# A gated-recurrence pass moved by half a slot to a slot, a row sum ahead of a copy from its bank, and one pair's casts on GpSimd

## The chip, the cores and the metric

One core of one Trainium2 chip runs the whole kernel. The metric is device time in microseconds (us) of one execution. A NeuronCore has a matrix engine (TensorE, PE in the profile; its weight loads are PEld), VectorE (DVE), ScalarE (ACT), GpSimd (POOL) and SyncE (SP, which here issues most DMAs). Each engine works through its own queue in order, and semaphores hold an instruction until what it needs is done. TensorE writes into PSUM, which has eight banks of 128 partitions by 512 fp32 numbers; VectorE and ScalarE read it, GpSimd does not.

## The reference, cut to what matters

One encoder layer over 1024 tokens of width 1024:

```
h     = layer_norm(x)
proj  = h @ w_in                     # 1024 -> 5120: q k v z_a u z_b g_a g_b
y_a   = neighbourhood_attention(q, k, v, rpb) * silu(z_a)
u     = centred_depthwise_conv(u)
for d in (forward, reverse):         # RG-LRU, 8 blocks of 64 channels
    r, i  = sigmoid(u @ w_gate + b_gate)
    a     = exp(-8 * softplus(-lam) * r)
    bx    = sqrt(1 - a*a) * i * u    # 1 instead of the root at the first position
    h_d   = scan: h[t] = a[t] * h[t-1] + bx[t]
y_b   = (h_0 + h_1) * silu(z_b)
m     = sigmoid(g_a + b0) * (y_a @ w_ba) + sigmoid(g_b + b1) * (y_b @ w_bb)
out   = layer_norm(2**0.25 * h + m @ w_out)
```

## The kernel before, in words

All matrix products are of fp32 data that is cut into a high and a low part (`hi`, `lo`), so each product is three matmuls (`mm3`, line 136, whose matmul is line 140). Two large stages, the combined input projection and the output projection, use a Strassen-Winograd scheme of seven products in place of eight. The order of all engines' queues is written out by hand.

**The projection stage** (about 81 to 420 us of the span). It handles 17 pairs of column blocks, p0 to p16; each pair has seven products, k0 to k6, in the order `a11 a12 s2 s1 s3 s4 a22`. One product is twelve matmuls and makes one slot: slot 7p+k. The loop over slots is at line 1162. In a slot, in this order: the results of the product before are taken out of PSUM (`evacuate`, line 1086); the high part of a weight for the next pair is cast (`s_hi`, line 474); the steps planned for position 0 of the slot; the squashings (`squash`, line 779); the product; the low parts of weights (`s_lo`, line 479); the stores; a weight sum on VectorE (`s_sum`, line 467); and the steps planned for position 1.

Products share banks: `s2`, `s3` and `a22` are added into the bank of `a11`, and `s4` into that of `s1`. So product k6 of a pair may start only when VectorE has read the state after k4 out of the bank. That read is line 776 (812 for keys, 767 for u), in `evacuate` of slot 7p+5, and appears in the profile as `c<-u,a` (a bank `c` from a copy `u` and the bank `a`; where `u` is taken, `up<-u,a`).

**The gate passes.** The recurrence has eight passes, one for each of four channel tiles and two directions (`gate_stage`, line 874), which begin at slots 21, 31, 42, 52, 63, 73, 84 and 94; they are called pass 0 to pass 7 here. The forward passes are the even ones. A pass consists of steps planned for a slot and a position counted from its beginning: `gates` (TensorE), `sigmoid` (ScalarE, line 892), `gated_input` (GpSimd, line 895), `decay` and `growth` (ScalarE, lines 898 and 902), `square` (ScalarE, line 905), `left` (VectorE, line 908, 1 + a*a times the tanh), `root` (ScalarE, line 911, with a table load), `tables` (ScalarE, line 914, which loads the sigmoid table again), `inputs` (a VectorE memset of one column, line 918, and GpSimd's product, line 919), `scan` (VectorE, line 924). A reverse pass goes on with `fetch`, `total` and two `gated`. The list of times is at lines 941 to 958. A convolution stage (`conv_stage`, line 831; its VectorE taps are line 843) runs beside it.

**Casts of weights.** Per pair, five high parts (`HI_POOL`, line 40) are cast on GpSimd, except for the pairs in `HI_ACT` (line 42), which ScalarE casts. Two low parts per pair are on GpSimd, the others on VectorE (line 134).

**The end.** The output projection ends with the four row blocks p0 to p3 of two halves r. `finished(p, r)` (line 1631) takes the mean and variance of a row block, normalises the two halves of the columns on ScalarE (`normal`, line 1637), scales them on GpSimd (`scaled_on`, line 1642) and stores them. For the block (2, 1) some work is inserted between the small steps of `newton` (line 1589) by `MEANWHILE` (line 1623): there it is a copy by ScalarE of the bank `banksX[3]` (line 1615). VectorE adds the same bank to a row block at line 1700 and takes its statistics at line 1587. Then come two half sums with the last product (`last_piece`, line 1626), the last normalisation (lines 1787 to 1799) and the last stores.

Of the kernel before, what the change touches and what calls it, by code (L numbers as in the profile page):

```python
# [13 lines left out]
ALU = mybir.AluOpType  # L14
# [24 lines left out]
LO_POOL = ("a11", "a22")  # L39
HI_POOL = ("a12", "s2", "s1", "s3", "s4")  # L40
FIRST_POOL = ("a22", "s4")
HI_ACT = (1, 2, 3, 16)
HELD = (18, 32, 37, 39, 60, 81)
U_PAIRS = (1, 6)
BLOCKS = (1, 0, 6, 4, 3, 2, 5, 7)
# [16 lines left out]
def tiled(ap, n):  # L62

    return ap[:, n * HALF:(n + 1) * HALF].rearrange("p (j r c) -> p j r c", r=GR, c=8)


def gridded(ap, n):

    return ap.rearrange("p (r j c) -> p j r c", r=GR, c=8)[:, 4 * n:4 * n + 4]
# [3 lines left out]
def encoder_kernel(ctx, tc, x, xt, gb1, gb, w_qk, w_v, w_s, w_ba, w_bb, w_gate, smalls, bias, w_out, out):  # L73
    nc = tc.nc
    V, A, G, PE, SP = nc.vector, nc.scalar, nc.gpsimd, nc.tensor, nc.sync
# [47 lines left out]
    def pair(pl, shape, name, **kw):  # L123
        return [pl.tile(shape, F32R, name=f"{name}_{c}", **({**kw, "tag": kw["tag"] + c} if "tag" in kw else kw))
                for c in "hl"]
# [348 lines left out]
    def s_hi(p, o):  # L474
        if p < N_PAIR:
            s_w[p, o] = pair(wsp, [P, 4, P], f"w{o}_{p}", tag="w" + o)
            (G.tensor_copy if p and o in HI_POOL and p not in HI_ACT else A.copy)(s_w[p, o][0][:], s_a[p, o])

# [349 lines left out]
    def at(slot, pos, f):  # L828
        todo.setdefault((slot, pos), []).append(f)
# [44 lines left out]
    def gate_stage(t, d, slot):  # L874
        g = {}

        def gates(b):
            uc, us, gw, _ = ucs[t]
            if b == 0:
                for c in "ria":  # L880
                    g[c] = lru.tile([P, S], F32, tag=c, name=f"{c}{t}_{d}")
            o = psd.tile([P, 2, HALF], F32, tag="gates", name=f"g{t}{d}{b}")
            for n in range(2):
                for z, w in enumerate(gw):
                    PE.matmul(o[:, n, :], w[:, 2 * d + b, :], us[b][:, n * HALF:(n + 1) * HALF], start=z == 0, stop=z == 1)  # L885
            g["o"] = o[:].rearrange("p n f -> p (n f)")

        def sigmoid(b, c):
            own, other = HALVES[b]
            src = own if c == "r" else other  # L890
            col = SM_GB + (d * 2 + b) * 4 + t
            A.activation(g[c][own], g["o"][src], AF.Sigmoid, bias=sm[src, col:col + 1])

        def gated_input():
            G.tensor_tensor(g["i"][:], g["i"][:], ucs[t][0][:], ALU.mult)

        def decay():
            A.activation(g["a"][:], g["r"][:], AF.Exp, scale=nsp[:, d * 4 + t:d * 4 + t + 1])

        def growth():  # L900
            w = g["w"] = lru.tile([P, S], F32, tag="wh", bufs=2, name=f"w{t}_{d}")
            A.activation(w[:], g["r"][:], AF.Tanh, scale=sp[:, d * 4 + t:d * 4 + t + 1])

        def square():
            A.activation(g["r"][:], g["a"][:], AF.Square)

        def left():
            V.scalar_tensor_tensor(g["w"][:], g["r"][:], 1.0, g["w"][:], ALU.add, ALU.mult)

        def root():  # L910
            A.activation(g["w"][:], g["w"][:], AF.Sqrt)

        def tables():
            A.activation(warm, eps_t, AF.Sigmoid)

        def inputs():
            first = S - 1 if d else 0
            V.memset(g["w"][:, first:first + 1], 1.0)
            G.tensor_tensor(g["w"][:], g["i"][:], g["w"][:], ALU.mult)

        def scan():
            st = -1 if d else 1
            w = g["w"]
            V.tensor_tensor_scan(w[:, ::st], g["a"][:, ::st], w[:, ::st], 0.0, ALU.mult, ALU.add)
            if d == 0:
                hsum[t] = w

        def fetch():
            for n in range(2):
                zs = g["out", n] = ev.tile([P, HALF], F32, tag="z", bufs=5, name=f"zs{t}_{n}")  # L930
                SP.dma_start(zs[:], zb_d[t][:, n * HALF:(n + 1) * HALF])

        def total():
            V.tensor_tensor(hsum[t][:], g["w"][:], hsum[t][:], ALU.add)

        def gated(n):
            zs = g["out", n]
            V.tensor_tensor(tiled(zs[:], 0), gridded(hsum[t][:], n), tiled(zs[:], 0), ALU.mult)
            SP.dma_start(yb_d[t][:, n * HALF:(n + 1) * HALF], zs[:])

        for b in range(2):
            at(slot + 2 * b, 1, lambda b=b: gates(b))
            for c in "ri":
                at(slot + 2 * b + 1, 1, lambda b=b, c=c: sigmoid(b, c))
        at(slot + 4, 0, gated_input)
        at(slot + 4, 1, decay)
        at(slot + 5, 1, growth)
        at(slot + 7, 0, square)
        at(slot + 8, 0, left)
        at(slot + 8, 1, root)  # L950
        at(slot + 9, 0, tables)
        at(slot + 9, 0, inputs)
        at(slot + 10, 1, scan)
        if d:
            at(slot + 10, 1, fetch)
            at(slot + 11, 1, total)
            for n in range(2):
                at(slot + 12 + n, 0, lambda n=n: gated(n))
# [203 lines left out]
    for slot in range(7 * N_PAIR + 4):  # L1162
        p, k = divmod(slot, 7)
# [331 lines left out]
    for slot in range(16):  # L1495
        j, n = divmod(slot, 2)
# [42 lines left out]
    zs, gbs = {}, {}  # L1539
# [35 lines left out]
    zp, banksX, banksW, stats = None, {}, {}, {}  # L1575
# [4 lines left out]
    def seen(p, r, n, src):  # L1580
        pieces = [slice(0, 256), slice(256, HALF)] if (p, r) == (3, 1) else [slice(0, HALF)]
        if (p, r) not in stats:
            stats[p, r] = small(f"st{p}{r}", 12 * len(pieces), f"st{len(pieces)}", 7)
        st = stats[p, r]
        for c, part in enumerate(pieces):
            c += n * len(pieces)
            V.bn_stats(st[:, 6 * c:6 * c + 6], src[:, part])
# [21 lines left out]
    def third_gained():  # L1609
        gained_in_bank(3)  # L1610
        A.copy(zs[2, 1, 0][:], banksX[2][:])
        yield

    def left_copied():
        A.copy(zs[3, 1, 0][:], banksX[3][:])
        yield

    def mean_var(p, r):
        mv = small(f"mv{p}{r}", 2, "mv", 2)
        V.bn_aggr(mv[:], stats[p, r][:].rearrange("p (c s) -> p c s", s=6))  # L1620
        return mv

    MEANWHILE = {(1, 1): lambda: (third_gained(), A), (2, 1): lambda: (left_copied(), V)}
    late_pieces = slice(0, 256), slice(256, HALF)

    def last_piece(c):
# [4 lines left out]
    def finished(p, r):  # L1631
        mv = mean_var(p, r)
        sd, ve = newton(mv, f"{p}{r}", *MEANWHILE.get((p, r), lambda: (iter(()), A))())
        A.activation(ve[:, 1:2], ve[:, 2:3], AF.Copy, scale=sd[:])

        def normal(dst, n, part=slice(0, HALF)):
            A.activation(dst[:, part], zs[p, r, n][:, part], AF.Identity, bias=ve[:, 1:2], scale=sd[:])  # L1637

        def scaled_on(n, *ops, part=slice(0, HALF)):
            z = zs[p, r, n][:, part]  # L1640
            for c in ops:
                G.tensor_tensor(z, z, gbs[c, n][:, part], (ALU.mult, ALU.add)[c])  # L1642

        def stored(n):
            SP.dma_start(out[p + 4 * r][:, halves[n]], zs[p, r, n][:])

        for n in range(2):
            if n == 1 and (p, r) in IN_BANK:
                normal(banksW[p], n)
                continue  # L1650
            normal(zs[p, r, n], n)
            if (p, r, n) == (2, 1, 1):
                for part in late_pieces:
                    scaled_on(n, 0, 1, part=part)
                    SP.dma_start(out[p + 4 * r][:, halves[n]][:, part], zs[p, r, n][:, part])
                continue
            scaled_on(n, 0, 1)
            stored(n)
# [3 lines left out]
    def gained_in_bank(p):  # L1662
        V.tensor_tensor(banksW[p][:], banksW[p][:], gbs[0, 1][:], ALU.mult)

    def shifted_from_bank(p, r):
        z = zs[p, r, 1]
        V.tensor_tensor(z[:], banksW[p][:], gbs[1, 1][:], ALU.add)
        SP.dma_start(out[p + 4 * r][:, halves[1]], z[:])
# [9 lines left out]
    def added(z, o):  # L1678
        V.tensor_tensor(z[:], z[:], o[:], ALU.add)
# [8 lines left out]
    def upper_right(p):  # L1688
        added(zs[p, 0, 1], banksW[p])
        seen(p, 0, 1, zs[p, 0, 1])  # L1690
        finished(p, 0)

    def lower_right(p):
        if p < 3:
            added(zs[p, 1, 1], banksX[p])
            seen(p, 1, 1, zs[p, 1, 1])
            if p == 2:
                shifted_from_bank(3, 0)
            return
        V.tensor_tensor(banksW[p][:], zs[p, 1, 1][:], banksX[p][:], ALU.add)  # L1700
        seen(p, 1, 1, banksW[p])

    def lower_left(p):
# [45 lines left out]
    for slot in range(16 + len(plan)):  # L1749
        j, n = divmod(slot, 2)  # L1750
# [137 lines left out]
```

## Time and profile before

| | us |
|---|---|
| median of 3 runs | 657.51 |
| lowest and highest | 657.47, 657.64 |
| the profiled execution, whole | 658.84 |
| its span, first to last instruction | 657.1 |
| busy in the span: TensorE / VectorE / ScalarE / GpSimd | 644.1 / 540.6 / 413.5 / 399.2 |
| mean granted TensorE clock | 0.997 |

A row of the timeline holds the start in us from the start of the span, the duration in us, the engine, the line, the operation, what is written from what with the shapes, and the count of merged instructions. In square brackets stands how long the engine was idle before it and what ended that. A row of the table by stretches holds the stretch, its length, the busy time of each engine with its instructions, the granted TensorE clock, the share of the DMA engines' time and what they moved. Durations come from one profiled execution, which took 1.33 us longer than the median run.

### The profile page before, as it was taken

What the parts mean: (1) busy time and instruction counts of PE and PEld (TensorE: products, weight loads), DVE (VectorE), ACT (ScalarE), POOL (GpSimd) and SP (SyncE); (2) the same over time, 40 slices, a digit from 0 to 9 for tenths busy, and PEclk for the clock granted to TensorE, in tenths of its full rate; (3) what the DMA queues carried; (4) which work ended last, traced back from release to release, by engine and by line L of the source; (5) the groups of instructions that cost most, each with busy time, mean ns of one, the idle gap of its engine ahead of it and who ended that gap; (6) DMA issues with size and microseconds to landing.
All of it is one profiled execution on the core that took longest, in us unless ns stands there. A gap on an engine that the chain in (4) does not pass through costs nothing.

```text
span 657.1 us, 9482 instructions
## 1 busy us (share of the span) xinstructions
PE 644.1 (98%) x3089; PEld 539.4 (82%) x3089; DVE 540.6 (82%) x849; ACT 413.5 (63%) x738; POOL 399.2 (61%) x326
## 2 busy tenths in 40 slices
PE   7999999999999999999999999999999999999994
PEld 6888888888878888888888888889888888888884
DVE  7988998995999799979988695277887875994776
ACT  5569554567776677777666745277777744574253
POOL 5559769933655576558556434012652649989957
PEclk9999999999999999999999999999999999999998
DMA  8674676433333233532362548797977288333033
GB/s 327 218 288 149 197 238 252 145 128 113 128 102 118 87 113 119 170 113 80 135 217 67 186 174 303 280 351 261 359 277 244 66 314 291 111 116 129 17 112 129
DMA packets 54065, 118.66 MB, mean 181 GB/s; under 512 B 5680, under 2 KB 10368, under 8 KB 52480
## 3 DMA queue, kind: packets, MB, share of 16 engines
q1 hardware_dynamic: 53696, 117.67, 51.9%
q8 instruction: 24, 0.39, 0.2%
q10 hardware_dynamic: 320, 0.40, 0.2%
q14 instruction: 25, 0.20, 0.1%
HBM read 82.36 MB, written 35.68 MB: 180 GB/s over the span
## 4 chain that ended last, share of the span: by engine, by line
PE 86%; DVE 6%; DMA 3%; ACT 2%; issue 1%; SPq 0%; DVEq 0%; ACTq 0%
PE a L140 32%; PE mb L140 13%; PE s L140 12%; PE x L140 6%; PE w L140 5%; PE v L413 4%; PE acc L1267 3%; PE s L1219 3%; PE pt L1241 3%; PE g L885 2%; PE q L140 2%; DMA v_d<-vs 1%; DMA wvsl<-in_w_v_dram 1%; DVE uc L843 1%; DVE ws_l L134 1%
## 5 line engine op out<-in xcount | busy, mean ns | idle before, releaser
L140 PE MATMUL a<-ht_h,ws_h 128*128 128x512 f32 x136 | 53.0, 389 | 0.0
L140 PE MATMUL a<-ht_h,ws_l 128*128 128x512 f32 x136 | 52.9, 389 | 0.0
L140 PE MATMUL a<-b_h,wa_h 128*128 128x512 f32 x136 | 52.9, 389 | 0.0
L140 PE MATMUL a<-b_h,wa_l 128*128 128x512 f32 x136 | 52.9, 389 | 0.0
L140 PE MATMUL a<-ht_l,ws_h 128*128 128x512 f32 x136 | 52.9, 389 | 0.0
L140 PE MATMUL a<-b_l,wa_h 128*128 128x512 f32 x136 | 52.9, 389 | 0.0
L1229 DVE CUSTOM_DVE_ANT_0 sc<-s,bias 128x384 f32<-128x384 f32 (+1 forms) x64 | 33.4, 522 | 19.8 <-PE s L1219 9.8
L1248 ACT CAST pt_h<-pt 128x384 fp32r<-128x384 f32 x64 | 29.0, 453 | 23.1 <-PE pt L1241 18.9
L993 POOL CAST wb_h<-wb 128x512 fp32r<-128x512 f32 x9 | 7.0, 781 | 58.3 <-DMA wb<-in_w_bb_dram 37.4
L1234 ACT ACTIVATE p<-sc,summ 128x384 f32<-128x384 f32 (+1 forms) x64 | 37.8, 591 | 5.5 <-DVE summ L1229 5.2
L140 PE MATMUL mb<-ya,wb_h 128*128 128x512 f32 x128 | 39.6, 389 | 0.0
L134 DVE TENSOR_TENSOR pt_l<-pt,pt_h 128x384 fp32r<-128x384 f32 x64 | 33.2, 519 | 1.8 <-ACT pt_h L1248 1.5
L413 PE MATMUL v<-wv,b_h 128*128 128x512 f32 x128 | 32.7, 397 | 1.1 <-ACT wv L203 0.7
L1219 PE MATMUL s<-ks,qs 128*128 128x384 f32 (+1 forms) x128 | 31.7, 329 | 0.0
L1642 POOL TENSOR_TENSOR z<-z,gb 128x512 f32<-128x512 f32 (+1 forms) x22 | 25.9, 1189 | 9.0 <-ACT z L1637 8.2
L1241 PEld LDWEIGHTS pt<-ident,p 128*128 128x128 f32 x176 | 22.9, 140 | 8.9 <-issue 0.9
L140 PEld LDWEIGHTS a<-ht_h,ws_h 128*128 128x128 f32 x136 | 25.5, 188 | 5.5 <-issue 0.2
L140 PEld LDWEIGHTS a<-ht_l,ws_h 128*128 128x128 f32 x136 | 25.5, 188 | 5.3
L140 PEld LDWEIGHTS a<-b_l,wa_h 128*128 128x128 f32 x136 | 25.5, 188 | 5.3
L140 PEld LDWEIGHTS a<-b_h,wa_l 128*128 128x128 f32 x136 | 25.5, 188 | 5.3
L140 PEld LDWEIGHTS a<-b_h,wa_h 128*128 128x128 f32 x136 | 25.5, 188 | 5.3
L140 PEld LDWEIGHTS a<-ht_h,ws_l 128*128 128x128 f32 x136 | 25.5, 188 | 5.2
(579 smaller groups left out, 2296.6 us busy)
## 6 DMA issues: line engine op xcount, KB each, us to landing
ks<-k_d SPq DMA_DIRECT2D x8, 1024.0 KB, 7.5
v_d<-vs SPq DMA_DIRECT2D x8, 512.0 KB, 3.3
q_d<-q SPq DMA_DIRECT2D x8, 512.0 KB, 3.0
ga_d<-ga SPq DMA_DIRECT2D x16, 256.0 KB, 2.0
gb_d<-gb SPq DMA_DIRECT2D x16, 256.0 KB, 2.7
k_d<-k SPq DMA_DIRECT2D x8, 512.0 KB, 3.5
qs<-q_d SPq DMA_DIRECT2D x8, 512.0 KB, 6.0
g<-gb_d SPq DMA_DIRECT2D x16, 256.0 KB, 6.1
```

What stands on the lines that cost most here:

```text
L134: eng.tensor_tensor(lo, full, hi.bitcast(F32), ALU.subtract)
L140: PE.matmul(o, a, b, start=first and i == 0, stop=last and i == len(prods) - 1, skip_group_check=not (first and last))
L413: PE.matmul(vos[i][:], a, wv[kind == "w"][k][:], start=vn[i] == 0, stop=vn[i] == 23)
L885: PE.matmul(o[:, n, :], w[:, 2 * d + b, :], us[b][:, n * HALF:(n + 1) * HALF], start=z == 0, stop=z == 1)
L993: G.tensor_copy(hi[:], st[:])
L1219: PE.matmul(o[:, :P * len(near(t))], q[:, t * P:(t + 1) * P], k[:, z, keys], start=z == 0, stop=z == 1)
L1229: V.tensor_tensor_reduce(s[:, :w], o[:, :w], heads[h][2][:, b0:b0 + w], -1.0, 3.0e38, ALU.add, ALU.min, accum_out=sums[h][0][:, t:t + 1])
L1234: A.activation(probs[h % 2][t][:], scs.pop((h, t))[:, :w], AF.Exp, bias=sums[h][0][:, t:t + 1], scale=-1.0, accum_out=sums[h][1][:, t:t + 1])
L1241: PE.transpose(tp[:, n * P:(n + 1) * P], probs[h % 2][t][:, z * P:(z + 1) * P], ident[:])
L1248: A.copy(pt[0][:, span(b)], tps[h, b][:, :P * len(near(b))])
L1267: PE.matmul(acc[n][:, lo - n * HALF:hi - n * HALF], vvs[h // 2][:, b, h % 2, :], pt[:, a:a + hi - lo], start=b in (1, 6) and z == 0, stop= ...
L1642: G.tensor_tensor(z, z, gbs[c, n][:, part], (ALU.mult, ALU.add)[c])
```

## The change

- In a gate pass `left` and `root` go from slot+8 to slot+9 (same positions), `tables` from slot+9 to slot+10, `inputs` from position 0 to position 1 of slot+9, and `scan` from position 1 of slot+10 to position 0 of slot+11.
- Pair 16 leaves `HI_ACT`: its five high casts go from ScalarE to GpSimd.
- At the end, VectorE's sum out of `banksX[3]` is placed in `finished(2, 1)` ahead of the large steps, and ScalarE's copy out of that bank between the normalisations of the two halves; before, the copy stood in `newton` and the sum behind `finished(2, 1)`.

```
-HI_ACT = (1, 2, 3, 16)
+HI_ACT = (1, 2, 3)
...
         at(slot + 7, 0, square)
-        at(slot + 8, 0, left)
-        at(slot + 8, 1, root)
-        at(slot + 9, 0, tables)
-        at(slot + 9, 0, inputs)
-        at(slot + 10, 1, scan)
+        at(slot + 9, 0, left)
+        at(slot + 9, 1, root)
+        at(slot + 10, 0, tables)
+        at(slot + 9, 1, inputs)
+        at(slot + 11, 0, scan)
...
-    def left_copied():
-        A.copy(zs[3, 1, 0][:], banksX[3][:])
-        yield
-
...
-    MEANWHILE = {(1, 1): lambda: (third_gained(), A), (2, 1): lambda: (left_copied(), V)}
+    MEANWHILE = {(1, 1): lambda: (third_gained(), A), (2, 1): lambda: (iter(()), V)}
...
+        if (p, r) == (2, 1):
+            V.tensor_tensor(banksW[3][:], zs[3, 1, 1][:], banksX[3][:], ALU.add)
         for n in range(2):
+            if (p, r, n) == (2, 1, 1):
+                A.copy(zs[3, 1, 0][:], banksX[3][:])
...
-        V.tensor_tensor(banksW[p][:], zs[p, 1, 1][:], banksX[p][:], ALU.add)
         seen(p, 1, 1, banksW[p])
```

## The prediction

> **What bounds the kernel now.** I read the page first, then the busy time by stretches, then the idle places of TensorE on the timeline.
>
> ```profile
> span 657.1 us, 9482 instructions
> PE 644.1 (98%) x3089; PEld 539.4 (82%) x3089; DVE 540.6 (82%) x849; ACT 413.5 (63%) x738; POOL 399.2 (61%) x326
> ```
>
> TensorE is idle for 13.0 us in all. By stretches:
>
> ```profile
> 0.00:20.00 20.00, 16.62 (x94) 13.20 (x95) 15.18 (x37) 11.59 (x23) 13.20 (x15) 1.00 0.85 317
> ...
> 135.00:200.00 65.00, 64.29 (x283) 52.91 (x283) 55.61 (x57) 48.08 (x60) 33.43 (x25) 1.00 0.39 130
> ...
> 646.00:657.10 11.10, 2.62 (x22) 2.42 (x21) 6.75 (x16) 2.63 (x6) 6.91 (x8) 0.85 0.45 162
> ```
>
> Of the 13.0 us, 3.38 lie in the start-up and 8.48 behind the last product. In the stretch of the gate passes only 0.71 is left, and it is one place. The timeline shows it (TensorE, then VectorE):
>
> ```profile
> 195.59 0.39 PE L140 MATMUL s<-b_l,ws_h 128*128 128x512 f32 x1
> 196.69 0.50 PE L140 MATMUL a<-ht_h,wa_h 128*128 128x512 f32 x1 [0.71 <-DVE c L776]
> ```
> ```profile
> 194.82 1.21 DVE L908 SCALAR_TENSOR_TENSOR w<-r,w 128x1024 f32<-128x1024 f32 x1
> 195.96 0.68 DVE L776 TENSOR_TENSOR c<-u,a 128x512 f32<-128x512 f32 x1
> ```
>
> Matmuls here follow each other at 64.29/283 = 0.23 us, so a start 1.10 us after the last one is a loss of 0.87. The first matmul of pair 5's k6 waited for VectorE's `c<-u,a`, which ended at 196.64, and directly ahead of that read stands pass 1's `left`. So TensorE is the bound, and the gate passes matter only where VectorE brings `c<-u,a` too late. What the change can win there is 0.87 us; what it can lose is not bounded by this, because the other pairs have little room. The room is the start of k6's first matmul less the end of `c<-u,a`, for the pairs whose `c` follows the scan of an even pass:
>
> ```profile
> 175.51 0.68 DVE L776 TENSOR_TENSOR c<-u,a 128x512 f32<-128x512 f32 x1
> ...
> 237.09 0.68 DVE L776 TENSOR_TENSOR c<-u,a 128x512 f32<-128x512 f32 x1
> ...
> 298.42 0.68 DVE L776 TENSOR_TENSOR c<-u,a 128x512 f32<-128x512 f32 x1
> ...
> 358.25 0.68 DVE L812 TENSOR_TENSOR c<-u,a 128x512 f32<-128x512 f32 x1
> ```
> ```profile
> 176.78 0.39 PE L140 MATMUL a<-ht_h,wa_h 128*128 128x512 f32 x1
> ...
> 238.53 0.39 PE L140 MATMUL a<-ht_h,wa_h 128*128 128x512 f32 x1
> ...
> 299.28 0.39 PE L140 MATMUL a<-ht_h,wa_h 128*128 128x512 f32 x1
> ...
> 360.07 0.39 PE L140 MATMUL a<-ht_h,wa_h 128*128 128x512 f32 x1
> ```
>
> That is 0.59 us at pair 4 (pass 0), 0.76 at pair 7 (pass 2), 0.18 at pair 10 (pass 4), 1.14 at pair 13 (pass 6).
>
> **The gate pass, odd passes.** In pass 1, `left` moves from the slot of k4 to that of k5 and leaves the place ahead of `c<-u,a` for the one behind it. The read starts 195.96 - 194.82 = 1.14 us earlier and would end at 195.50, before TensorE wants the bank at 195.59 + 0.23 = 195.82. What pass 0 costs (0.15 to 0.6, below) is carried over, since VectorE was busy for 30.26 of the 30.40 us before this place.
>
> ```profile
> 166.20:196.60 30.40, 29.78 (x132) 24.33 (x130) 30.26 (x24) 22.37 (x28) 19.39 (x14) 1.00 0.36 118
> ```
>
> So the end lies at 195.65 to 196.1. The stall shrinks from 0.87 to between 0 and 0.3; gain 0.57 to 0.87.
>
> **The gate pass, even passes.** These stand three products earlier in a pair: `left` moves from the slot of k1 to that of k2, and there behind the evacuation `a<-u,a`. Pass 4, the one with least room, before (VectorE, GpSimd, ScalarE):
>
> ```profile
> 283.01 1.46 DVE L908 SCALAR_TENSOR_TENSOR w<-r,w 128x1024 f32<-128x1024 f32 x1 [1.89 <-ACT r L905]
> ...
> 286.86 0.70 DVE L776 TENSOR_TENSOR a<-u,a 128x512 f32<-128x512 f32 x1 [1.79 <-PE a L140]
> ...
> 288.20 0.06 DVE L918 MEMSET w<- 128x1 f32 x1
> 288.78 2.89 DVE L134 TENSOR_TENSOR wa_l<-a_11f,wa_h 128x512 fp32r<-128x512 f32 x1
> ...
> 293.30 2.69 DVE L924 TENSOR_TENSOR_SCAN w<-a,w 128x1024 f32<-128x1024 f32 x1
> ```
> ```profile
> 282.09 1.30 POOL L134 TENSOR_TENSOR wa_l<-a_10f,wa_h 128x512 fp32r<-128x512 f32 x1 [2.76 <-ACT wa_h L477]
> 286.88 0.62 POOL L477 CAST wa_h<-a_11f 128x512 fp32r<-128x512 f32 x1 [3.49 <-issue]
> 288.41 2.72 POOL L919 TENSOR_TENSOR w<-i,w 128x1024 f32<-128x1024 f32 x1 [0.91 <-DVE w L918]
> ```
> ```profile
> 287.08 1.06 ACT L911 ACTIVATE w<-w 128x1024 f32<-128x1024 f32 x1
> ```
>
> Two things are to be seen. First, `left` was done in time that VectorE had to spare: it waited 1.89 us for ScalarE's square and 1.79 us for TensorE. Ahead of `a<-u,a` this time cannot be saved for later, so removing the wait for the square wins nothing, and a `left` behind the evacuation is added to the way to `c`. Second, VectorE and GpSimd keep each other out when both read two operands from SBUF. `left` took 1.46 here and 1.21 in pass 1; here GpSimd's `wa_l` held until 283.39, and `left` ended 1.08 later. GpSimd's product of `inputs` ended at 291.13, and VectorE's `wa_l`, 2.89 long, ended 0.54 after that.
>
> Now the same stretch after the change. With GpSimd first: its cast ends at 287.50, its `wa_l` (1.30) at 288.80; VectorE's `left` ends 1.08 later, 289.88; ScalarE's root (1.06, with 0.1 for the semaphore, an estimate from 288.14, where the root ended, to the memset at 288.20) at 291.04; a weight sum of 0.6 on VectorE (it lies between the memset and the `wa_l` above) fits before that; the memset, queued behind it, waits for the root until 291.10, and behind the memset wait VectorE's `wa_l`, the next weight sum and the scan. `wa_l` gets in first (0.6, to 291.7). GpSimd's product starts 0.21 after the memset and takes 2.72, to 294.03; the weight sum ends 0.54 later, and the scan starts at 294.5: 1.2 later than 293.30. With VectorE first: `left` ends at 288.8, GpSimd's `wa_l` at 290.1, the sum at 290.6, memset 290.65, product at 293.6, scan at 294.1: 0.8 later. So 7.2 to 7.65 us lie between the starts of `a<-u,a` and of the scan. What follows the scan up to `c` is unchanged, so the shift of 0.8 to 1.2 arrives there, and with a room of 0.18 pair 10 stalls for 0.6 to 1.0.
>
> ScalarE's root now waits for a `left` that ends at 288.8 to 289.9. Queued behind it on ScalarE are the copy of the bank that product k4 adds to, `tables`, a squashing and the start of the convolution. The copy (0.6) can be done by 291.7, and k4 starts 24 matmuls and 4 gate matmuls before k6, at 299.28 - 28 x 0.23 = 292.9: cost 0, with a room of 1.2.
>
> Which comes first is decided within 0.1 us. The page "SBUF — State Buffer" of the Trainium skill, section "Who interferes with whom", says that issue order decides: the later of the two blocks fully until the first has finished. The durations of `left` agree with it; by its rule GpSimd, free at 287.50, would go first, and the sum would stand at its upper end.
>
> For the other even passes I use the same 7.2 to 7.65:
>
> ```profile
> 164.36 0.70 DVE L776 TENSOR_TENSOR a<-u,a 128x512 f32<-128x512 f32 x1 [1.19 <-PE a L140]
> ...
> 171.41 2.69 DVE L924 TENSOR_TENSOR_SCAN w<-a,w 128x1024 f32<-128x1024 f32 x1
> ...
> 226.11 0.70 DVE L776 TENSOR_TENSOR a<-u,a 128x512 f32<-128x512 f32 x1 [1.34 <-PE a L140]
> ...
> 231.97 2.69 DVE L924 TENSOR_TENSOR_SCAN w<-a,w 128x1024 f32<-128x1024 f32 x1
> ```
>
> Pass 0 took 7.05 before: shift 0.15 to 0.6 against a room of 0.59, stall 0. Pass 2 took 5.86: shift 1.3 to 1.8 against 0.76, stall 0.55 to 1.05. Pass 6 with pass 4's shift, 0.8 to 1.2 against 1.14: 0 to 0.05. With pair 10 that is 1.15 to 2.1 of new stalls, less 0.57 to 0.87: net +0.3 to +1.5. I take +0.95, near the middle, since the order at the port may differ from pass to pass. Odd passes 3, 5 and 7 have no stall to lose and gain room. `tables` follows the root and costs ScalarE what it did. No DMA moves.
>
> **Pair 16's casts.**
>
> ```profile
> 395.70 0.69 DVE L776 TENSOR_TENSOR c<-u,a 128x512 f32<-128x512 f32 x1 [1.13 <-PE a L140]
> ```
>
> Five casts go from ScalarE to GpSimd, where one took 0.62 (the cast at 286.88). VectorE idles 1.13 us before pair 15's read, which covers a collision with one cast or two; without that cover each would cost TensorE up to 0.6. Taken as 0, with 0 to 0.1 kept for the range.
>
> **The end.** (VectorE and ScalarE, TensorE, then the issues of the last stores.)
>
> ```profile
> 645.84 0.59 ACT L1615 COPY z<-x 128x512 f32<-128x512 f32 x1 [0.69 <-PE x L140]
> 646.46 0.70 DVE L1700 TENSOR_TENSOR w<-z,x 128x512 f32<-128x512 f32 x1 [0.65 <-ACT z L1615]
> 646.66 1.52 ACT L1637 ACTIVATE z<-z,ve,sd 128x512 f32<-128x512 f32 x2
> 648.85 0.43 DVE L1628 TENSOR_TENSOR x<-z,y 128x256 f32<-128x256 f32 x1
> ```
> ```profile
> 648.34 0.28 PE L140 MATMUL y<-t4l,a22h 128*128 128x256 f32 x1
> ```
> ```profile
> 653.25 0.33 SPq L1655 DMA_DIRECT2D out_dram<-z  x1
> 653.59 0.37 ACTq L1799 DMA_DIRECT2D out_dram<-z  x1
> 653.67 0.41 SPq L1799 DMA_DIRECT2D out_dram<-z  x1
> ```
>
> VectorE's sum starts 0.62 us earlier, at 645.84. ScalarE's copy moves behind the first normalisation: that ends near 646.95 (some 0.5 earlier, as most of the copy's 0.59 is out of its way), the copy near 647.55, and the first half sum can follow at once, before its old time. But the second half sum needs TensorE's last matmul, which ends at 648.62: it can start at 648.67, not 0.62 but 0.18 earlier. And the last store on SP stands behind one that waits for GpSimd and is issued at 653.25, which nothing here makes earlier; only ScalarE's store moves. Gain between 0 and 0.18; I take 0.05.
>
> **Sum.** +0.95 - 0.05 = +0.9 us. On the profiled execution: 658.84 to 659.7; on the median: 657.51 to 658.4 us.
>
> **The rivals.**
> - *The stall goes and none comes.* VectorE gets ahead of GpSimd at the port in passes 2 and 4, and GpSimd's later `inputs` fall where VectorE reads PSUM. For it: the wait of the memset for the root falls away in odd passes. Against it: even the low ends leave 0.6 and 0.55. Price -0.87 and up to -0.1 at the end: 656.6 us. Chance 0.24.
> - *Slower: the lateness is carried on.* GpSimd is first in every even pass (1.05 and 1.0 at pairs 7 and 10), pair 5 keeps 0.3, and VectorE, which idles only once per even pass, takes the rest of the shift into the next pair. It decides from the point where the shift that is left over exceeds a pair's room (0.18 to 1.14 above); I price one such overrun at 0.3, the middle between none and 0.6 for one collision. 1.05 + 1.0 + 0.3 + 0.3 - 0.87 = +1.8, less 0.05: about 659.2 us. For it: GpSimd's cast was free 0.1 before VectorE; against it: `left` behind `c` gives back 1.14 in each odd pass. Chance 0.26.
> - *Faster beyond 0.2%.* It needs 1.3 us, more than 0.87 + 0.18 together. Chance 0.05.
>
> **How the numbers follow.** 0.2% (1.3 us) is about what a measurement of this kernel can tell from no change. The forecast, chance 0.45, has its own range from 657.51 + 0.3 - 0.18 = 657.6 to 657.51 + 1.5 = 659.0, nearly all of it inside the 0.2%, which ends at 658.8; the first rival is inside it too. Same 0.69, slower 0.26, faster 0.05. The range reaches down to the first rival's 656.6 and up to 659.3, a little beyond the second.
>
> **What would show it.** Right: k6's first matmul of pair 5 no longer waits 0.71; new waits of TensorE for `c<-u,a` at about 238.5 and 299.3; `left` in even passes starting right behind `a<-u,a` and ending after a GpSimd instruction; VectorE's idle time before that `a<-u,a` grown. The second half sum starts right behind the last matmul. Wrong: `c<-u,a` at pairs 7 and 10 no later than before relative to k5's product; TensorE waiting for ScalarE, which now stands at the root until `left` is done; an end that moves by more than 0.2.

## The result and the profile after

The changed kernel takes 660.51 us (median of 5 runs, 660.04 to 660.71), beside 657.58 for the kernel before in runs beside it: the ratio is 1.0043, with a 95% interval of 1.0032 to 1.0054. It is 2.9 us slower, and lies above the range.

The two profiled executions differ by less, 660.04 against 658.84. The reason is the start-up, which nothing in the change touches: the first matmul of pair 4's k6 comes at 175.37 after and at 176.78 before. From that matmul to the last one it is 649.74 - 175.37 = 474.37 us after and 648.34 - 176.78 = 471.56 before, 2.81 more; behind the last matmul 8.56 and 8.76, 0.20 less. So the profiles account for 2.6 of the 2.9 us; the rest is within the interval.

Where the 2.81 lie, the busy time by stretches of the kernel after says (the second number is the length, the third TensorE's busy time):

```profile
80.00:200.00 120.00, 120.00 (x530) 99.04 (x529) 105.75 (x122) 76.23 (x105) 77.64 (x72) 1.00 0.47 160
200.00:260.00 60.00, 59.68 (x263) 49.11 (x262) 54.81 (x51) 42.05 (x52) 37.64 (x25) 1.00 0.29 100
260.00:320.00 60.00, 58.41 (x257) 47.76 (x256) 54.05 (x52) 41.56 (x51) 34.28 (x26) 1.00 0.33 111
320.00:380.00 60.00, 59.50 (x262) 48.74 (x261) 47.62 (x54) 39.02 (x52) 34.71 (x25) 1.00 0.51 164
```

Up to 200 us the row shows no idle time of TensorE: the stall at pair 5 is gone. From 200 on it loses 0.32, 1.59 and 0.50. The places, on TensorE's timeline after (each time the last matmul before the gap and the first behind it):

```profile
236.06 0.39 PE L885 MATMUL g<-us,gw_l 128*128 128x512 f32 x1
236.77 0.50 PE L140 MATMUL a<-ht_h,wa_h 128*128 128x512 f32 x1 [0.32 <-DVE c L776]
...
273.84 0.39 PE L140 MATMUL a<-ht_l,ws_h 128*128 128x512 f32 x1
274.96 0.47 PE L140 MATMUL s<-b_h,ws_h 128*128 128x512 f32 x1 [0.73 <-ACT u L1104]
...
298.40 0.39 PE L885 MATMUL g<-us,gw_l 128*128 128x512 f32 x1
299.65 0.50 PE L140 MATMUL a<-ht_h,wa_h 128*128 128x512 f32 x1 [0.86 <-DVE c L776]
...
336.72 0.39 PE L140 MATMUL a<-ht_l,ws_h 128*128 128x512 f32 x1
337.61 0.47 PE L140 MATMUL s<-b_h,ws_h 128*128 128x512 f32 x1 [0.50 <-ACT u L1104]
```

Matmuls should start 0.23 apart. What a gap is longer than that, together with the matmul behind it that comes 0.1 late, is the loss:

| wait at | before | after | foreseen |
|---|---|---|---|
| pair 5 k6, for VectorE's `c<-u,a` | 0.98 | 0 | 0 to 0.3 |
| pair 4 k6 | 0 | 0.11 | 0 |
| pair 7 k6, `c<-u,a` | 0 | 0.58 | 0.55 to 1.05 |
| pair 10 k6, `c<-u,a` | 0 | 1.12 | 0.6 to 1.0 |
| pair 13 k6 | 0 | 0.18 | 0 to 0.05 |
| pair 9 k5, for ScalarE's copy of `s` | 0 | 0.97 | not foreseen |
| pair 12 k5, for ScalarE's copy of `s` | 0 | 0.74 | not foreseen |

The first five rows come to 0.11 + 0.58 + 1.12 + 0.18 - 0.98 = +1.0, close to the +0.95 of the prediction. That they agree so closely is in part luck, since the single rows lie 0.2 below to 0.3 above the middle of what was foreseen. The last two rows add 1.7.

Pass 4 after, in the same order as it was shown before (VectorE, GpSimd):

```profile
286.20 0.70 DVE L776 TENSOR_TENSOR a<-u,a 128x512 f32<-128x512 f32 x1 [4.95 <-PE a L140]
286.81 2.36 DVE L908 SCALAR_TENSOR_TENSOR w<-r,w 128x1024 f32<-128x1024 f32 x1
...
290.32 0.06 DVE L918 MEMSET w<- 128x1 f32 x1 [0.56 <-ACT w L911]
290.37 0.69 DVE L134 TENSOR_TENSOR wa_l<-a_11f,wa_h 128x512 fp32r<-128x512 f32 x1
290.98 2.89 DVE L472 TENSOR_TENSOR s_11f<-a_11f,s_11f 128x512 f32<-128x512 f32 x1
293.80 2.69 DVE L924 TENSOR_TENSOR_SCAN w<-a,w 128x1024 f32<-128x1024 f32 x1
```
```profile
286.79 1.29 POOL L134 TENSOR_TENSOR wa_l<-a_11f,wa_h 128x512 fp32r<-128x512 f32 x1
290.53 2.80 POOL L919 TENSOR_TENSOR w<-i,w 128x1024 f32<-128x1024 f32 x1 [2.44 <-DVE w L918]
```

The idle time ahead of `a<-u,a` has grown from 1.79 to 4.95 us, and `left` stands behind it. GpSimd's `wa_l` starts 0.02 us ahead of `left` and holds it until 288.08; `left` ends 1.09 later. From the start of `a<-u,a` to that of the scan it is 293.80 - 286.20 = 7.60 us, against 6.44 before.

The waits in the stage say the same in sums. First the kernel before (VectorE, ScalarE), then the kernel after; the columns are us in total, times, the longest:

```profile
DVE w L908 <- ACT r L905: 7.2, 5, 2.3
DVE a L776 <- PE a L140: 7.1, 6, 1.9
...
ACT w L911 <- DVE w L908: 5.9, 3, 3.1
```
```profile
DVE a L776 <- PE a L140: 13.1, 6, 5.0
...
ACT w L911 <- DVE w L908: 24.5, 8, 3.7
```

VectorE's wait of 7.2 us for the square is gone, and in its place VectorE waits 6.0 us longer for TensorE, just ahead of the work that is now late.

The end after: TensorE's last matmul, VectorE's second half sum, the last issue on SP.

```profile
649.74 0.28 PE L140 MATMUL y<-t4l,a22h 128*128 128x256 f32 x1
```
```profile
650.05 0.43 DVE L1624 TENSOR_TENSOR x<-z,y 128x256 f32<-128x256 f32 x1 [0.21 <-PE y L140]
```
```profile
655.08 0.41 SPq L1798 DMA_DIRECT2D out_dram<-z  x1
```

The half sum now follows the start of the last matmul by 0.31 in place of 0.51. SP's last store follows it by 5.34, before 5.33: unmoved.

### The profile page after: what moved, and what is told of

Its sections match the earlier page's. It is cut to its first block, busy times and chain, and to the rows that moved or that the text cites. A ratio compares the mean times of both kernels' runs of the same rounds, so it can differ in the third digit from the quotient of the medians.

```text
span 658.3 us, 9480 instructions
## 1 busy us (share of the span) xinstructions
PE 644.9 (98%) x3089; PEld 539.4 (82%) x3089; DVE 542.2 (82%) x849; ACT 409.6 (62%) x733; POOL 406.7 (62%) x331
## 4 chain that ended last, share of the span: by engine, by line
PE 83%; DVE 10%; issue 3%; ACT 3%; DVEq 0%
PE a L140 26%; PE mb L140 13%; PE s L140 10%; PE v L413 7%; PE x L140 6%; PE w L140 5%; PE acc L1267 3%; PE q L140 3%; PE s L1219 3%; PE pt L1241 3%; DVE ws_l L134 2%; DVE uc L843 1%; PE g L885 1%; DVE w L908 1%; DVE w L924 1%
## 5 line engine op out<-in xcount | busy, mean ns | idle before, releaser
L919 POOL TENSOR_TENSOR w<-i,w 128x1024 f32<-128x1024 f32 x8 | 20.7, 2586 | 20.7 <-DVE w L918 20.7
```

## The experiments

Theory A: the forward passes (even) put VectorE late, because `left` stands behind the evacuation; the lateness reaches `c<-u,a` of the same pair and is carried on to pairs 9 and 12. Theory B: the waits for ScalarE at pairs 9 and 12 come from the reverse passes (odd), where `root` waits for a later `left`. Theory C: the casts or the end cost something. The ratios below are against the kernel before on the same chip, with their 95% intervals.

**The gate pass alone.** The kernel before with the five moved `at` lines.

> Only the gate passes' steps are moved; the casts and the end are as before. Theory A (the forward passes put VectorE late) and theory B (the reverse passes hold up ScalarE) both expect all of the loss here and the 0.2 us of the end missing: +2.9 to +3.3 us against before, with TensorE's waits for ScalarE's copy at pairs 9 and 12 and for VectorE at pairs 7 and 10. Theory C (the five casts on GpSimd cost something in the last third) expects clearly less, under +2.3.

Measured 661.24 against 658.18 us, 1.0053 (1.0040 to 1.0067), +3.1. TensorE's waits in the stage: 3.7 us, at the same pairs as after the whole change. C is out as a cause of the loss.

**The casts and the end alone.** The kernel after with the five old `at` lines.

> The gate passes are as before; the casts of pair 16 and the end are changed. A and B: -0.1 to -0.3 us, all of it from the second half sum starting right behind the last matmul; pair 5's wait of 0.7 is still there. C: slower than before by 0.3 or more.

Measured 658.12 against 658.18, 0.9999 (0.9990 to 1.0008): no difference that this can resolve. Its profile has pair 5's wait and no other, and 8.47 us behind the last matmul. In the eight profiles with the new end that stretch is 8.47 to 8.56, in the four with the old end 8.69 to 8.91: the end gains some 0.2.

**The reverse passes alone, the forward passes alone.** The kernel before, with the change made for one direction:

```
+        if d:                      # the other kernel: if not d
+            at(slot + 9, 0, left)
+            at(slot + 9, 1, root)
+            at(slot + 10, 0, tables)
+            at(slot + 9, 1, inputs)
+            at(slot + 11, 0, scan)
+        else:
+            at(slot + 8, 0, left)
...
```

> Only the reverse passes (odd) are moved. A: pair 5's stall is gone and nothing comes in its place, -0.8 to -1.1 us. B: the waits for ScalarE's copy at pairs 9 and 12 come with this half of the change, 0.9 and 0.7, so that the sum is +0.5 to +0.9.

> Only the forward passes (even) are moved. A: the stalls of 0.5 at pair 7, 0.9 at pair 9, 1.0 at pair 10 and 0.7 at pair 12 are here, and pair 5's stall stays or grows by what pass 0 is late: +2.6 to +4.5 us. B: only pairs 7 and 10 stall, +1.3 to +2.0.

The reverse passes alone: 657.22 against 658.18, 0.9989 (0.9980 to 0.9997), -1.0 us. Two short gaps of under 0.1 are left in the stage. The forward passes alone: 663.59, 1.0085 (1.0071 to 1.0099), +5.4 us. A's range for it ended at 4.5. Its profile has 6.0 us of waits, at pairs 4, 5, 7, 8, 9, 10, 11, 12 and 13. B is out: the half that it blames is the half that gains. Together the two halves cost 3.1, not 5.4 - 1.0 = 4.4, since the moved reverse pass absorbs some of the lateness: in its old place its own `left` stands ahead of `c<-u,a`, and pair 8 waits as well (TensorE, then VectorE, forward passes alone):

```profile
257.28 0.39 PE L140 MATMUL s<-b_l,ws_h 128*128 128x512 f32 x1
258.32 0.50 PE L140 MATMUL a<-ht_h,wa_h 128*128 128x512 f32 x1 [0.65 <-DVE w L918]
```
```profile
255.43 1.63 DVE L908 SCALAR_TENSOR_TENSOR w<-r,w 128x1024 f32<-128x1024 f32 x1
...
257.58 0.68 DVE L776 TENSOR_TENSOR c<-u,a 128x512 f32<-128x512 f32 x1
...
258.27 0.06 DVE L918 MEMSET w<- 128x1 f32 x1
```

The row of TensorE names the memset as the releaser. But the memset writes nothing that k6 uses; the read out of k6's bank ended at 258.26, at the same moment, and is what k6 waited for: a releaser is inferred, and here two candidates ended together.

**`left` and `root` early, the rest late.** The kernel after, with

```
-        at(slot + 9, 0, left)
-        at(slot + 9, 1, root)
+        at(slot + 9 if d else slot + 8, 0, left)
+        at(slot + 9 if d else slot + 8, 1, root)
```

> The changed kernel, but in the forward passes left and root stand in their old slots; tables, inputs and scan stay moved. If left behind the evacuation is what makes VectorE late, the waits at pairs 7, 9, 10, 12 and 13 fall from 3.6 us in sum to under 0.6, and the time is 657.0 to 657.8, no slower than before. If the later inputs and scan do it, most of the 3.6 stays: 659.5 or more.

Measured 656.50 against 657.49, 0.9984 (0.9976 to 0.9993): 1.0 us faster than before, and 0.5 below the lower end of what was expected. TensorE has one gap of 0.06 in the stage. So of the forward pass's five moved steps it is `left` with its root, and not `inputs` and `scan`, that makes the loss.

**ScalarE's squashing out of the way.** The copy at pair 9's k5 is late in ScalarE's queue behind two sigmoids, and these behind a squashing that waits for VectorE. ScalarE, kernel after:

```profile
267.92 0.59 ACT L1102 COPY u<-a 128x512 f32<-128x512 f32 x1 [2.61 <-PE a L140]
271.24 0.69 ACT L781 ACTIVATE ga<-a,smh 128x512 f32<-128x512 f32 x1 [2.73 <-DVE a L776]
271.96 1.11 ACT L892 ACTIVATE r<-g,sm 64x1024 f32<-64x1024 f32 x1
273.10 1.11 ACT L892 ACTIVATE i<-g,sm 64x1024 f32<-64x1024 f32 x1
274.23 0.59 ACT L1104 COPY u<-s 128x512 f32<-128x512 f32 x1
```

The experiment puts the squashing behind that copy at pairs 9 and 12:

```
-        squashes = rest[:1]
+        squashes = kept_back + rest[:1]
+        kept_back = []
+        if done in ((9, 1), (12, 1)):
+            squashes, kept_back = [], rest[:1]
```

> The changed kernel, but at pairs 9 and 12 ScalarE's squashing of the result that VectorE brings late stands one slot later, behind the copy that product k5 waits for. If ScalarE was late only because it stood waiting for VectorE there, the waits at pairs 9 and 12 (1.7 us with the slow matmul behind each) are gone and nothing else moves: 1.4 to 1.8 us faster than the changed kernel. If ScalarE is late by its own work, they stay within 0.4.

The waits for the copy are gone as expected, but the time is 661.36 against 657.49, 1.0059 (1.0045 to 1.0073): slower, not faster. The wait came back one product later, at k6, and longer (1.49 at pair 9, 1.28 at pair 12). TensorE, then GpSimd and VectorE of that kernel:

```profile
276.73 0.39 PE L140 MATMUL s<-b_l,ws_h 128*128 128x512 f32 x1
278.35 0.50 PE L140 MATMUL a<-ht_h,wa_h 128*128 128x512 f32 x1 [1.23 <-DVE c L776]
```
```profile
272.52 2.39 POOL L895 TENSOR_TENSOR i<-i,uc 128x1024 f32<-128x1024 f32 x1
```
```profile
272.60 2.86 DVE L472 TENSOR_TENSOR s_10f<-a_10f 128x512 f32<-128x512 f32 x1
```

The sigmoids came earlier, so GpSimd's product of them did too, and started 0.08 us ahead of a weight sum on VectorE, which took 2.86 for 0.68. So the copy was late because the squashing ahead of it waited for VectorE, as expected. But the new wait stems from a collision that the edit itself brought about, and what the waits at k5 cost by themselves cannot be read from this run.

**GpSimd out of `left`'s way.** The kernel after, with GpSimd's low part of the next pair's first weight held back by a slot in the forward passes:

```
-HELD = (18, 32, 37, 39, 60, 81)
+HELD = (18, 30, 32, 37, 39, 51, 60, 72, 81, 93)
```

> The changed kernel, but in the forward passes GpSimd's low part of the next pair's first weight is held back by one slot, behind inputs, so that GpSimd is free while VectorE does left. If the two keep each other out, left takes 1.21 in place of up to 2.3, inputs starts about 1 us earlier, and the waits fall from 3.7 us to between 0.3 and 1.5: 1.5 to 3.5 us faster than the changed kernel. If left is simply on the way, by its own 1.2 us, the gain is under 0.5.

Measured 659.36 against 657.49, 1.0028 (1.0017 to 1.0038). By the ratios that is 0.0015, 1.0 us, better than the changed kernel: between what the two readings expected. The profile shows why. `left`, the scan, the low part behind it and `c<-u,a` (VectorE), then the weight that was held back (GpSimd), in pass 4:

```profile
286.91 1.22 DVE L908 SCALAR_TENSOR_TENSOR w<-r,w 128x1024 f32<-128x1024 f32 x1
...
292.76 2.69 DVE L924 TENSOR_TENSOR_SCAN w<-a,w 128x1024 f32<-128x1024 f32 x1
295.38 1.72 DVE L134 TENSOR_TENSOR ws_l<-s_11f,ws_h 128x512 fp32r<-128x512 f32 x1
...
298.56 0.68 DVE L776 TENSOR_TENSOR c<-u,a 128x512 f32<-128x512 f32 x1
```
```profile
293.27 3.27 POOL L134 TENSOR_TENSOR wa_l<-a_11f,wa_h 128x512 fp32r<-128x512 f32 x1
```

`left` takes 1.22 in place of 2.36, as the exclusion has it. From `a<-u,a`, which starts at 286.31, to the scan it is 6.45 us, as long as in the kernel before (6.44), though `left` now stands on this way. But the held weight then meets the scan and takes 3.27 in place of 1.29, and VectorE's low part behind the scan takes 1.72 in place of 1.03. So `c<-u,a` follows `a<-u,a` by 12.25 us, against 11.56 before and 12.71 after, and 2.9 us of waits stay, at pairs 7, 9, 10 and 12. The 0.69 us over the kernel before lie behind the scan, where the held weight now runs, so what `left` costs by its own length alone this run does not show.

**One forward pass at a time.** The kernel after, with the change in the forward direction for one pass alone (`if d or slot == 42`, or 63).

> The changed kernel, but of the forward passes only pass 2 is moved; 0, 4 and 6 are as before. If VectorE's lateness of one forward pass is carried on to the next pair but one, the waits are 0.6 at pair 7 and 0.5 to 1.0 at pair 9, and none at pairs 10 and 12: +0.1 to +0.7 us against before, since pair 5's stall of 1.0 is gone. If the wait at pair 9 belongs to pass 4, which begins there, only pair 7 waits: -0.9 to -0.3.

> The changed kernel, but of the forward passes only pass 4 is moved. Carried on: 1.1 at pair 10 and 0.4 to 0.8 at pair 12, none at pairs 7 and 9; +0.2 to +0.9 us against before. Not carried on: pair 10 alone, or pair 10 with pair 9: -0.1 to +0.2 or +0.9.

Pass 2 alone: 658.83 against 658.21, 1.0008 (0.9999 to 1.0017). TensorE waits 1.12 at pair 7 (0.6 was expected) and 0.71 at pair 9, and nowhere else for more than 0.1.

```profile
238.25 0.50 PE L140 MATMUL a<-ht_h,wa_h 128*128 128x512 f32 x1 [0.86 <-DVE c L776]
...
276.20 0.47 PE L140 MATMUL s<-b_h,ws_h 128*128 128x512 f32 x1 [0.48 <-ACT u L1111]
```

Pass 4 alone: 658.91, 1.0010 (1.0001 to 1.0019), with 1.12 at pair 10 and 0.73 at pair 12. Each of the two passes makes two stalls, the second 38 us behind the first. Passes 0 and 6 were not tried alone. The carrying on is shown by this together with the next run: beside the one even pass only the reverse passes, the casts and the end are changed here, and these alone make no wait at pair 9 or 12.

**Reverse passes, casts and end.** The kernel after with the forward passes put back.

> The changed kernel with the forward passes put back: reverse passes, casts and end as changed. TensorE has under 0.2 us of waits in the stage, and the end is 0.2 shorter: 0.9 to 1.3 us faster than the kernel before. A theory in which the casts or the end cost something expects less than 0.7.

Measured 656.54 against 657.49, 0.9987 (0.9978 to 0.9995), -0.95 us, with 0.3 us lost in the stage (under 0.2 was expected), of which 0.2 is at pair 15. It and the kernel with `left` early, which was on the same chip, beat both kernels, and are not to be told apart.

## Why the prediction was wrong, step by step

- **The bound** was right: TensorE, and VectorE's `c<-u,a` where it comes too late.
- **Odd passes**: pair 5's stall went altogether, where 0 to 0.3 was left to it. The reverse half alone gains 1.0 us.
- **Even passes, the direct term**: right in mechanism, and in size but for the late second matmul, 0.1 at each stall, which the sum did not have: pair 10's gap alone costs 1.02, beside 0.6 to 1.0 foreseen, and 1.12 with that matmul. Both orders at the port were seen, and each fell as it was worked out. In pass 4 GpSimd came first (286.79 against 286.81) and the scan followed `a<-u,a` by 7.60 us (7.65 foreseen); in pass 2 of the changed kernel VectorE came first, at 224.47 against 224.74, and it was 7.05 (7.2 foreseen), with a stall of 0.58 at pair 7. With pass 2 alone GpSimd was first there, at 225.39 against 225.41, and the stall was 1.12. Both agree with the rule of issue order on the page "SBUF — State Buffer" of the Trainium skill, section "Who interferes with whom". That GpSimd would go first in each pass was not so.
- **The step that failed** is "Odd passes 3, 5 and 7 have no stall to lose and gain room". It ended the lateness of an even pass with the stall at its own pair. But a stall of 0.58 gives back only a part of the shift of 1.19 in pass 2 (7.05 less 5.86), and VectorE has no idle time in which to make up for the rest: it was busy for 33.62 of the 33.80 us from 236.70 to 270.50. At pair 9 the kernel before had `a<-u,a` at 270.28, 0.72 us after ScalarE's copy of k2 at 269.56; the kernel after has it at 270.52, 2.60 us after 267.92:

```profile
269.56 0.59 ACT L1102 COPY u<-a 128x512 f32<-128x512 f32 x1 [2.61 <-PE a L140]
```
```profile
270.28 0.68 DVE L776 TENSOR_TENSOR a<-u,a 128x512 f32<-128x512 f32 x1
```
```profile
270.52 0.69 DVE L776 TENSOR_TENSOR a<-u,a 128x512 f32<-128x512 f32 x1
```

  So VectorE was 1.88 us later against TensorE there. That is more than the 0.6 that pair 7's stall left over. The reverse passes moved alone make 0.22 of it (0.94 after the copy in place of 0.72, with no stall). The rest came up on the way, where VectorE's late instructions met GpSimd's. Two of them, a convolution tap and a product of pass 3:

```profile
237.23 2.31 DVE L843 SCALAR_TENSOR_TENSOR uc<-up,sm,uc 128x1024 f32<-128x1024 f32 x1
...
266.37 2.31 DVE L934 TENSOR_TENSOR w<-w,w 128x1024 f32<-128x1024 f32 x1
```

  They took 1.63 and 1.22 with the forward passes put back. GpSimd had started 0.27 and 0.50 us ahead of them, and they ended 1.08 us after it. In between some of the lateness was given back (from `a<-u,a` to `c<-u,a` of pair 8 it is 6.02 us, against 6.87 with the forward passes put back). The way to pair 12 was not followed row by row.

  ScalarE's squashing waits for the result of this `a<-u,a`, the sigmoids stand behind the squashing and the copy that k5 needs behind the sigmoids. I had looked at ScalarE's queue behind the waiting root, in the even pass, and not at this one. The second rival had the lateness that is carried on, though not the way through ScalarE, and priced it at one overrun of 0.3; it was two, of 0.97 and 0.74.
- **Pair 16's casts**: no wait of more than 0.1 appeared in the changed kernel. With the forward passes put back, pair 15's k6 lost 0.2, behind a weight sum on VectorE that took 1.09 beside a cast (0.68 without), so the 0 to 0.1 that was kept for the casts was too little there.
- **The end**: 0.05 was taken, 0.2 was measured. The half sum came as foreseen, and SP's last store stayed as foreseen. ScalarE's last store is issued 5.09 us after the start of the last matmul in place of 5.25, which is about the gain; that the end waits for this one is not shown.

The changed sum is 1.0 + 1.7 - 0.2 = +2.5 us, beside 2.9 measured; 0.1 of the difference is shorter gaps, the rest lies between the profiled execution and the median.

## What to carry to other kernels

An engine's idle time ahead of a wait is where work that is not urgent costs nothing: taking a wait out by moving the work behind the next one can lose more than the wait was long. When a queue has no idle time, follow a delay through it until the next idle time, and at each step through the queues of the engines that wait for it; a price for the first stall alone is not the price. Late instructions also meet other instructions of an engine that they keep out, or that keeps them out, so the lateness can grow on the way. If a move is tried in two kinds of places, try each kind alone: here one half gained 1.0 us and the other lost 5.4.

## What was not expected of the hardware

Which of VectorE and GpSimd gets in first was decided by 0.02 us in pass 4 and, where it was moved alone, in pass 2 (by 0.27 there in the changed kernel). In pass 2 it is worth 0.5 us at TensorE. The blocked instruction can be either: GpSimd's `wa_l` took 1.29, 2.28 or 3.27. And a stall of TensorE costs 0.1 us more than its gap, since the second matmul behind it starts 0.30 to 0.34 after the first, not 0.23.
